# Attention scores as products over 128 rows, with stacked queries and doubled keys

## The chip, the core and the metric

The kernel runs on one core of a Trainium2 chip. Its engines are TensorE (PE in the profile, with its weight loads as PEld), VectorE (DVE), ScalarE (ACT), GpSimd (POOL) and SyncE (SP, which only issues DMAs here). The metric is the device time of one execution in microseconds, the median of some runs.

## What is computed

Two blocks of layers work on 512 positions of width 1024, in float32. The first block has two hybrid layers. Each normalises its input, multiplies it with `w_in`, and runs three kinds of attention over 64-wide heads: differential attention (4 heads with two score maps each), stick-breaking attention (8 heads) and forgetting attention (8 heads). The second block is a float32 mixture: a Hyena layer, an expert layer with 16 experts, a sliding-window attention (SWA) layer with 16 query and 4 key heads, and a second expert layer. Cut to the lines that matter here:

```python
# hybrid layer, query tile i of 128 rows, keys up to its end
s = einsum('bhcqd,bhckd->bhcqk', q[..., q0:q1, :], k[..., :q1, :]) * 64 ** -0.5   # differential
z = einsum('bhqd,bhkd->bhqk', q[:, :, q0:q1], k[:, :, :q1]) * scale               # stick-breaking, forgetting
logits = z + cum_log_f[..., q0:q1, None] - cum_log_f[..., None, :q1]              # forgetting
# SWA, a block of 128 queries: 256 context keys and a band of up to three key blocks
s_ctx = einsum('bqgrd,bkgd->bgrqk', q_b, k_c) * scale
s_loc = einsum('bqgrd,bkgd->bgrqk', q_b, k_b) * scale
```

## The kernel before

**Numbers in two parts.** TensorE multiplies values of a shortened float32 type. Every float32 operand is therefore kept as a high part h and a low part l with h + l = x; `split` (L227 on ACT, L228 on DVE) makes them: ACT copies x into h, DVE subtracts h from x. A product is three matmuls, hh + lh + hl (`mm3`, L93 to L95). The product of the two low parts is left out.

**Scores in the hybrid layers.** A head has 64 features, so a tile of 128 rows holds two heads. `scores` (L584 to L587) takes the 64 rows `rs` of one head and sums four matmuls into one PSUM tile `s`, w = 128, 256, 384 or 512 columns wide for query tile i = 0 to 3; the fourth, over all 128 rows, adds the mask:

```python
nc.tensor.matmul(s[:, :w], q[rs, 0, qs], k[rs, 0, :w], start=True, stop=False)
nc.tensor.matmul(s[:, :w], q[rs, 1, qs], k[rs, 0, :w], start=False, stop=False)
nc.tensor.matmul(s[:, :w], q[rs, 0, qs], k[rs, 1, :w], start=False, stop=False)
nc.tensor.matmul(s[:, i * P:w], self.identr, self.masks[:, mask, :], start=False, stop=True)
```

A layer has 6 units (two of each kind), a unit two pairs of heads, a pair two heads, a head four query tiles: 96 such blocks a layer, 192 in all. The forgetting heads also spread a row of `cum` over 128 rows with a matmul over 40 rows (L690).

**Order of the work in a layer.** `pair(u, j)` projects queries, keys and gates of a pair of heads (24 matmuls of 512 columns each, `proj_f`), splits q and k (L430 and L431, or L227 and L228, after a rotation in `rope_split` for the differential kind) and keeps them in the tiles `q` (3 buffers) and `k` (2). `attend(u, j)` runs scores, softmax and values of that pair. `interleave` weaves the attention of one pair with the projections of the next and the output projection of the unit before (`project_out`). Tile's scheduler then sets each engine's order from these dependencies; every engine works its own list in order.

**Beside it: the adaptive weights.** `between` weaves in `ada_piece`: for the second block's modulation vectors, a 1 MB tile `araw` (one buffer) is loaded on SP's queue, and POOL multiplies its 8 rows with a column and adds them up (L804 once, then L801 and L802 seven times) into `aacc` (4 buffers). There are 24 such sums in layer 0 and 32 in layer 1. `ada_flush` has TensorE turn each `aacc` into a column (`psA`, L821), at a place in TensorE's list that lies up to three sums later. The tile `araw` shares its buffer with the gain rows that a layer's end reads, so the first piece of layer 1 is loaded when layer 0 has ended.

**A layer's end.** `finish` squares, normalises and adds each of the four row tiles (ACT's squares into `xs`, L244, are 128x1024). `xs` lies in the buffers of `q`.

**SWA.** Queries are already stacked there: of a head's 128 rows one half holds the high part, the other the low part, and the keys `kT` stand on both halves. `swa_scores` (L1944, L1945) takes the first product over 128 rows, which gives hh + lh, and the second over the 64 rows of the high part, which gives hl. There are 144 pairs of such matmuls: 96 of 256 columns, 32 of 128, 16 of 512. SWA lies between the two expert layers, whose weights (about 190 MB each) are streamed.

Of the kernel before, what the change touches and what calls it, by code (L numbers as in the profile page):

```python
# [22 lines left out]
P = 128  # L23
D = 1024
S = 512
# [154 lines left out]
class Net:  # L180
# [91 lines left out]
    def first_block(self, before, after, between=lambda n: iter(()), behind=lambda: None):  # L272
# [3 lines left out]
        with ExitStack() as ex:  # L276
            self.pv = self.hx.enter_context(self.pool("pv"))
            self.pA = ex.enter_context(self.pool("pA"))
            pA = self.pA
# [12 lines left out]
            self.sel = pA.tile([40, 8], F32R, name="sel")  # L292
            nc.vector.tensor_tensor(self.sel, self.ident[0:40, 0:8], self.ident[0:40, 32:40], op=ALU.add)
# [32 lines left out]
    def hybrid(self, l, before, after, between):  # L326
# [5 lines left out]
        lv = pA.tile([1, 4, 64], F32, tag="lv", name="lv")  # L332
        nc.sync.dma_start(lv, io["diff_lambda"][l].unsqueeze(0))
        lp = pA.tile([1, 2, 64], F32, tag="lp", name="lp")
# [22 lines left out]
        def forget():  # L357
# [12 lines left out]
            self.cum = pA.tile([40, S], F32R, tag="cum", name="cum")  # L370
# [44 lines left out]
        def pair(u, j):  # L415
# [77 lines left out]
        def finish(tts):  # L493
            for tt in tts:
# [3 lines left out]
                xs = pA.tile([P, D], F32, tag="q", name="xs", bufs=3)  # L498
# [34 lines left out]
    def context_norm(self):  # L533
# [6 lines left out]
        for tt in range(2):  # L540
            x = cx[:, tt, :]
            scr = self.pA.tile([P, D], F32, tag="q", name="cs", bufs=3)
# [22 lines left out]
    def rope_split(self, dst, a):  # L565
# [10 lines left out]
        self.split(dst[:, 0, :], dst[:, 1, :], t1)  # L576

    def scores(self, q, k, r0, i, mask):
# [3 lines left out]
        rs = slice(r0, r0 + 64)  # L582
# [40 lines left out]
    def diff_head(self, q, k, vt, j, gt, sub, nlam, y):  # L623
# [4 lines left out]
        def exps(i):  # L628
            w = (i + 1) * P
            e, zs = [], []  # L630
            for c in range(2):
                s = self.scores(q, k, 64 * c, i, 0)
# [44 lines left out]
    def pair64(self, kind, q, k, vt, j, gt, y, head0, groups):  # L677
# [6 lines left out]
        def exps(hh, g, i):  # L684
            w = (i + 1) * P
            if kind == "f" and i == groups[0][0]:
                n = cols.stop
                cb = self.ps.tile([P, S], F32, tag="s", name="cb", bufs=3)
                sel = self.sel[:, head0 + hh:head0 + hh + 1].to_broadcast([40, P])
# [1458 lines left out]
```

## Time and profile before

| | |
|---|---|
| median of 3 runs | 3364.06 us (3361.09 to 3375.61) |
| the profiled execution | 3359.41 us |
| its span, first to last instruction | 3357.5 us |
| hybrid layer 0, layer 1 | about 150 to 680, 680 to 1250 us |
| SWA attention | about 2540 to 2800 us |
| busy: PE, DVE, ACT, POOL | 2995.8, 2215.3, 1504.6, 1103.9 us |

The durations below belong to the profiled execution. Busy times of PE overcount, because the end of a matmul is modelled and successive ones overlap: the distance from start to start is what a matmul costs the engine. Waits are named by what came last. TensorE's clock is 2.4 GHz at a granted share of 1.00 and 1.2 GHz at 0.50.

### The profile page before, as it was taken

The page shows a single profiled execution, that of the slowest core. Times are in us where ns is not written, and L with a number is a line of the kernel's source. Part 1 is how long each engine was busy: PE and PEld are TensorE (multiplying, and loading weights), DVE is VectorE, ACT ScalarE, POOL GpSimd, SP SyncE. Part 2 cuts the span into 40 slices and gives each one's busy share as a digit, 9 for nine tenths or more (in the row PEclk, how much of TensorE's full clock was granted, in tenths as well). Part 3 has the DMA queues.
Part 4 walks back from the last instruction along what each step waited for, and adds up shares of the span by engine and source line. Part 5 has one row for each costly group of instructions (what it writes and reads, how often), then busy time and mean ns, then how long its engine had stood idle before and what let it go on. Part 6 is the DMA issues. An engine that isn't in the chain of part 4 may idle for free. (4 is left out here: it accounts for less than half of the span.)

```text
span 3357.5 us, 42248 instructions
## 1 busy us (share of the span) xinstructions
PE 2995.8 (89%) x15148; PEld 2169.4 (65%) x15148; DVE 2215.3 (66%) x4023; ACT 1504.6 (45%) x2649; POOL 1103.9 (33%) x1310
## 2 busy tenths in 40 slices
PE   7999999899999988998886999999798995976776
PEld 4777778687777768888775677766576773322222
DVE  8676776776677588878867899998776665100002
ACT  5345664544465353332322788877654652000001
POOL 4374665167766622113332012120203231000000
PEclk9999999999899989999997999999997987998988
DMA  5432222323233334553466999999431016999996
GB/s 175 150 112 89 79 91 82 120 95 107 88 126 114 126 114 135 163 163 115 154 221 259 335 387 382 390 373 366 148 107 58 13 51 255 403 403 404 404 398 267
DMA packets 289513, 673.23 MB, mean 201 GB/s; under 512 B 16352, under 2 KB 151759, under 8 KB 289304
## 3 DMA queue, kind: packets, MB, share of 16 engines
q1 hardware_dynamic: 267592, 604.50, 49.1%
q0 software_dynamic: 18256, 58.70, 5.9%
q10 hardware_dynamic: 3456, 7.34, 0.6%
q8 instruction: 120, 1.97, 0.2%
q14 instruction: 89, 0.73, 0.1%
HBM read 618.49 MB, written 51.99 MB: 200 GB/s over the span
## 5 line engine op out<-in xcount | busy, mean ns | idle before, releaser
L228 DVE TENSOR_TENSOR mwl<-raww,mwh 128x1024 fp32r<-128x1024 f32 x384 | 461.3, 1226 | 56.9 <-ACT mwh L227 53.9
L227 ACT ACTIVATE mwh<-raww 128x1024 fp32r<-128x1024 f32 x384 | 405.2, 1060 | 147.1 <-PE psg L94 61.9
L802 POOL TENSOR_TENSOR aacc<-aacc,aprod 128x256 f32<-128x256 f32 x392 | 328.7, 839 | 31.7
L1503 PE MATMUL psg<-raww,xt 128*64 128x512 f32 x1024 | 259.4, 649 | 88.5 <-DMA raww<-in_moe_w_gate_dram 48.5
L801 POOL TENSOR_SCALAR aprod<-araw,cvec 128x256 f32<-128x256 f32 x392 | 259.0, 661 | 64.5 <-DMA araw<-in_ada_w_dram 29.8
L1528 DVE TENSOR_TENSOR a<-psg,a 128x512 f32<-128x512 f32 x16 | 11.1, 692 | 362.8 <-ACT a L1527 362.8
L1503 PEld LDWEIGHTS psg<-raww,xt 128*64 128x64 f32 x1024 | 73.6, 147 | 261.1 <-issue 136.9
L93 PE MATMUL acc<-hTh,wh 128*128 128x512 f32 x576 | 231.8, 402 | 0.0
L94 PE MATMUL acc<-hTh,wl 128*128 128x512 f32 x576 | 227.7, 395 | 1.5 <-DVE wl L228 1.5
L95 PE MATMUL acc<-hTl,wh 128*128 128x512 f32 x576 | 227.8, 396 | 0.0
L1527 ACT ACTIVATE a<-psg 128x512 f32<-128x512 f32 x16 | 9.6, 597 | 364.7 <-PE psg L1503 364.7
L228 DVE TENSOR_TENSOR wl<-raw,wh 128x1024 fp32r<-128x1024 f32 x106 | 140.4, 1325 | 42.3 <-ACT wh L227 42.3
L1440 POOL DMA_INDIRECT xe<-hrows,idx x16 | 21.5, 1345 | 390.8 <-PE psC L1432 366.6
L1518 POOL DMA_INDIRECT xe<-hrows,idx x16 | 15.7, 983 | 355.8 <-PE psC L1510 319.9
L1503 PE MATMUL psd<-raww,at 128*64 128x512 f32 x512 | 118.1, 609 | 13.5 <-DVE ye L1540 8.2
L227 ACT ACTIVATE wh<-raw 128x1024 fp32r<-128x1024 f32 x106 | 111.6, 1053 | 30.9 <-PE accv L94 19.7
L94 PEld LDWEIGHTS acc<-hTh,wl 128*128 128x128 f32 x576 | 109.0, 189 | 21.5 <-DVE wl L228 2.1
L95 PEld LDWEIGHTS acc<-hTl,wh 128*128 128x128 f32 x576 | 108.7, 189 | 21.8
L93 PEld LDWEIGHTS acc<-hTh,wh 128*128 128x128 f32 x576 | 109.0, 189 | 19.9 <-issue 0.4
L93 PE MATMUL accv<-wvh,hTh 128*128 128x256 f32 x384 | 111.7, 291 | 0.0
L94 PE MATMUL accv<-wvh,hTl 128*128 128x256 f32 x384 | 110.9, 289 | 0.7 <-DVE hTl L228 0.7
L95 PE MATMUL accv<-wvl,hTh 128*128 128x256 f32 x384 | 109.8, 288 | 0.3 <-DVE wvl L228 0.3
(631 smaller groups left out, 8995.0 us busy)
## 6 DMA issues: line engine op xcount, KB each, us to landing
raww<-in_moe_w_gate_dram SPq DMA_DIRECT2D x128, 1024.0 KB, 9.9
raww<-in_moe_w_up_dram SPq DMA_DIRECT2D x127, 1024.0 KB, 10.8
raww<-in_moe_w_down_dram SPq DMA_DIRECT2D x125, 1024.0 KB, 18.5
raw<-in_w_in_dram SPq DMA_DIRECT2D x48, 1024.0 KB, 5.5
araw<-in_ada_w_dram SPq DMA_DIRECT2D x36, 1024.0 KB, 5.0
spec<-sp SPq DMA_DIRECT2D x24, 512.0 KB, 3.1
rawo<-in_w_out_dram SPq DMA_DIRECT2D x12, 1024.0 KB, 7.2
raw<-in_hy_w_in_dram SPq DMA_DIRECT2D x12, 1024.0 KB, 5.3
```

What stands on the lines that cost most here:

```text
L93: nc.tensor.matmul(out, ah, bh, start=start, stop=False)
L94: nc.tensor.matmul(out, al, bh, start=False, stop=False)
L95: nc.tensor.matmul(out, ah, bl, start=False, stop=stop)
L227: self.split_act = self.nc.scalar.activation(h, src, AF.Copy).ins
L228: (eng or self.nc.vector).tensor_tensor(l, src, h.bitcast(F32), op=ALU.subtract)
L801: nc.gpsimd.tensor_scalar(prod, raw[:, c, :], col, 0.0, op0=ALU.mult, op1=ALU.add)
L802: nc.gpsimd.tensor_tensor(acc, acc, prod, op=ALU.add)
L1440: m.gather = nc.gpsimd.indirect_dma_start(out=xe, out_offset=None, in_=m.hrows[:, :], in_offset=bass.IndirectOffsetOnAxis(ap=idx[:, e:e + ...
L1503: nc.tensor.matmul(out[64 * hf:64 * hf + 64], lhs[:, c % 4, 64 * (c // 4):64 * (c // 4) + 64], raw[:, cc, hf * 512:hf * 512 + 512], start= ...
L1518: m.gather = nc.gpsimd.indirect_dma_start(out=xe, out_offset=None, in_=halves(m.hrows), in_offset=bass.IndirectOffsetOnAxis(ap=idx[:, e:e ...
L1527: self.last_other = nc.scalar.activation(a, gu[:, 0, :], AF.Silu).ins
L1528: nc.vector.tensor_tensor(a, gu[:, 1, :], a, op=ALU.mult)
```

## The change

- In the hybrid layers `stack` writes the queries of each head over all 128 rows, the high part on the head's own 64 rows and the low part on the other 64, and `twice` writes each head's keys on both halves, high and low. `scores` then takes two matmuls over 128 rows and the mask: (h; l) against kh, and (h; l) against kl, which also adds the product of the low parts.
- `q` has 2 buffers in place of 3; `k` has twice the size. `cum` and `sel` have 128 rows.
- In SWA the second product is taken over 128 rows, too.
- To make room, `lo` goes: the scratch half is kept in `yv`. `lv`, `lp` and `hrow` move into the buffers of `x`; `xs` (a layer's end) and `pp` (Hyena) move from the buffers of `q` to those of `y`, the attention outputs that the last output projection reads.

```diff
-            self.cum = pA.tile([40, S], F32R, tag="cum", name="cum")
+            self.cum = pA.tile([P, S], F32R, tag="cum", name="cum")
...
-            q = pA.tile([P, 2, S], F32R, tag="q", name="q", bufs=3)
-            k = pA.tile([P, 2, S], F32R, tag="k", name="k", bufs=2)
+            q = pA.tile([P, 2, S], F32R, tag="q", name="q", bufs=2)
+            k = pA.tile([P, 2, 2, S], F32R, tag="k", name="k", bufs=2)
...
                 if kind == "a":
-                    self.rope_split(dst, a)
-                elif n == 0:
-                    nc.scalar.activation(dst[:, 0, :], a, AF.Copy, scale=0.125)
-                    nc.vector.scalar_tensor_tensor(dst[:, 1, :], a, 0.125, dst[:, 0, :].bitcast(F32),
-                                                   op0=ALU.mult, op1=ALU.subtract)
+                    a = self.roped(dst if n == 0 else dst[:, 0], a)
+                if n == 0:
+                    self.stack(dst, a, None if kind == "a" else 0.125)
                 else:
-                    self.split(dst[:, 0, :], dst[:, 1, :], a)
+                    self.twice(dst, a)
...
-                xs = pA.tile([P, D], F32, tag="q", name="xs", bufs=3)
+                xs = pA.tile([P, D], F32, tag="y", name="xs", bufs=3)
...
+    def stack(self, q, a, scale=None):
+        for i in range(2):
+            h, l = slice(64 * i, 64 * i + 64), slice(64 - 64 * i, 128 - 64 * i)
+            nc.scalar.activation(q[h, i, :], a[h], AF.Copy, scale=1.0 if scale is None else scale)
+            if scale is None:
+                nc.vector.tensor_tensor(q[l, i, :], a[h], q[h, i, :].bitcast(F32), op=ALU.subtract)
+            else:
+                nc.vector.scalar_tensor_tensor(q[l, i, :], a[h], scale, q[h, i, :].bitcast(F32),
+                                               op0=ALU.mult, op1=ALU.subtract)
+    def twice(self, k, a):
+        for i in range(2):
+            h, o = slice(64 * i, 64 * i + 64), slice(64 - 64 * i, 128 - 64 * i)
+            self.split(k[h, i, 0, :], k[h, i, 1, :], a[h])
+            if i == 0:
+                nc.scalar.activation(k[o, i], k[h, i].bitcast(F32), AF.Copy)
+            else:
+                nc.vector.tensor_copy(k[o, i], k[h, i].bitcast(F32))
...
-        nc.tensor.matmul(s[:, :w], q[rs, 0, qs], k[rs, 0, :w], start=True, stop=False)
-        nc.tensor.matmul(s[:, :w], q[rs, 1, qs], k[rs, 0, :w], start=False, stop=False)
-        nc.tensor.matmul(s[:, :w], q[rs, 0, qs], k[rs, 1, :w], start=False, stop=False)
+        for x in range(2):
+            nc.tensor.matmul(s[:, :w], q[:, hh, qs], k[:, hh, x, :w], start=x == 0, stop=False)
...
-            lo = pA.tile([P, S], F32, tag="lo", name="lo", bufs=1)
-            nc.scalar.activation(lo[0:64, cols], o[64:128, cols], AF.Copy)
-            nc.vector.tensor_tensor(yv[rows, cols], o[0:64, cols], lo[0:64, cols], op=ALU.add)
+            nc.scalar.activation(yv[64:128, cols], o[64:128, cols], AF.Copy)
+            nc.vector.tensor_tensor(yv[rows, cols], o[0:64, cols], yv[64:128, cols], op=ALU.add)
...
-            nc.tensor.matmul(o, q[rq, r, qs], kT[rq, g, 1, ks], start=False, stop=n + k == len(order) or n + k == 4)
+            nc.tensor.matmul(o, q[:, r, qs], kT[:, g, 1, ks], start=False, stop=n + k == len(order) or n + k == 4)
```

Since a scheduler sets the order, the built programs were compared, too. Three places matter. TensorE's list, layer 0, unit 0, second pair, last query tile (`s` is a score block, `acc` a projection, `psP` a transpose, `psA` one of the adaptive columns); before:

```order
L95 MATMUL acc<-hTl,wh 128x512
L584 MATMUL s<-k,q 128x512
L585 MATMUL s<-k,q 128x512
L586 MATMUL s<-k,q 128x512
L587 MATMUL s<-masks,identr 128x128
L93 MATMUL acc<-hTh,wh 128x512
```

After:

```order
L93 MATMUL acc<-hTh,wh 128x512
L606 MATMUL s<-k,q 128x512 x2
L607 MATMUL s<-masks,identr 128x128
L606 MATMUL s<-k,q 128x512 x2
L607 MATMUL s<-masks,identr 128x128
L640 MATMUL psP<-ident,e 128x128 x2
```

A block is three matmuls where it was four; the two heads' blocks now follow each other here. Of the 56 adaptive columns of the two layers, each stands behind the same share of the score blocks as before, to about 1 in 100.

ACT's list, layer 0, unit 3, keys of the first pair (`k<-acc` is the high part, `wh` a weight split, `e` softmax, `pt` a transposed weight tile, `sg` the gate); before:

```order
L701 ACTIVATE e<-e,one 128x512
L227 ACTIVATE k<-acc 128x512
L227 ACTIVATE wh<-raw 128x1024
L742 ACTIVATE lo<-o 64x512
L227 ACTIVATE pt<-psP 128x2x128
```

After:

```order
L721 ACTIVATE e<-e,one 128x512
L227 ACTIVATE k<-acc 64x512
L227 ACTIVATE wh<-raw 128x1024
L761 ACTIVATE yv<-o 64x512
L583 ACTIVATE k<-k 64x1024
L227 ACTIVATE k<-acc 64x512
L227 ACTIVATE pt<-psP 128x2x128
L736 ACTIVATE e<-e 128x512
L557 ACTIVATE sg<-acc 128x512
```

One operation has become three, and the copy of the first head's keys (L583) needs DVE's subtraction first. On DVE one subtraction has become two and a copy (CAST `k<-k 64x1024`). On TensorE, in all 24 pairs, at least 28 matmuls (the 24 of the gate's projection among them) stand between the end of the keys' projection and the first score that reads them.

ACT's list at the end of layer 0 (`xs,ss` is a square, `y` the last attention output, `yv` or `lo` its halves, `wvh` a weight split for layer 1); before:

```order
L244 ACTIVATE xs,ss<-yacc 128x1024
L227 ACTIVATE y<-yv 128x128
L233 ACTIVATE rs<-ss,eps 128x1
L235 ACTIVATE rs<-rs 128x1
L244 ACTIVATE xs,ss<-yacc 128x1024
L742 ACTIVATE lo<-o 64x128
```

After:

```order
L244 ACTIVATE xs,ss<-yacc 128x1024
L227 ACTIVATE y<-yv 128x128
L233 ACTIVATE rs<-ss,eps 128x1
L235 ACTIVATE rs<-rs 128x1
L761 ACTIVATE yv<-o 64x128 x2
L227 ACTIVATE y<-yv 128x128
L227 ACTIVATE wvh<-raw 128x1024
L244 ACTIVATE xs,ss<-yacc 128x1024 x2
```

The squares of the second and third row tile have moved behind the last attention output and a weight split. SP's and POOL's lists of loads and sums keep their order but for single rows; POOL's 448 multiplications and additions of layer 1 are the same.

## Rows read from the trace of the kernel before

**Rows 1.** By stretch: us, busy (count) of PE, PEld, DVE, ACT, POOL; PEclk, DMA share, GB/s.

```profile
150.00:600.00 450.00, 444.73 (x2369) 354.78 (x2368) 320.59 (x666) 240.95 (x498) 270.10 (x366) 1.00 0.30 94
690.00:1180.00 490.00, 468.17 (x2403) 371.46 (x2403) 323.55 (x658) 242.23 (x498) 351.20 (x480) 0.96 0.34 111
2580.00:2700.00 120.00, 115.10 (x595) 84.83 (x594) 83.49 (x266) 78.03 (x198) 40.60 (x41) 0.99 0.05 19
```

**Rows 2.** Timeline of PE, blocks of 512 columns: start, duration in us, line, operands.

```profile
803.21 0.50 PE L584 MATMUL s<-k,q 64*128 64x512 f32 x1
803.56 0.39 PE L585 MATMUL s<-k,q 64*128 64x512 f32 x1
803.79 0.39 PE L586 MATMUL s<-k,q 64*128 64x512 f32 x1
804.11 0.33 PE L587 MATMUL s<-masks,identr 128*128 128x128 f32 x1
804.37 0.49 PE L584 MATMUL s<-k,q 64*128 64x512 f32 x1
```

**Rows 3.** Timeline of PE, score blocks of 128 columns.

```profile
785.60 0.32 PE L584 MATMUL s<-k,q 64*128 64x128 f32 x1
785.76 0.27 PE L585 MATMUL s<-k,q 64*128 64x128 f32 x1
785.88 0.27 PE L586 MATMUL s<-k,q 64*128 64x128 f32 x1
...
786.34 0.33 PE L584 MATMUL s<-k,q 64*128 64x128 f32 x1
```

**Rows 4.** Timeline of PE, SWA: score products, then products with the values.

```profile
2600.18 0.38 PE L1945 MATMUL sc<-kT,qw 64*128 64x256 f32 x1
2600.49 0.39 PE L1944 MATMUL sc<-kT,qw 128*128 128x256 f32 x1
2600.81 0.38 PE L1945 MATMUL sc<-kT,qw 64*128 64x256 f32 x1
...
2602.09 0.28 PE L1845 MATMUL ow<-ptl,vt 128*128 128x256 f32 x1
2602.21 0.28 PE L1845 MATMUL ow<-pth,vt 128*128 128x256 f32 x1
```

**Rows 5.** Groups on DVE, 60 to 1250 us: form, count, busy us, mean ns, idle before.

```profile
L228 DVE TENSOR_TENSOR wl<-raw,wh 128x1024 fp32r<-128x1024 f32 x73 | 98.0, 1343 | 40.2 <-ACT wh L227 40.2
...
L228 DVE TENSOR_TENSOR k<-acc,k 128x512 fp32r<-128x512 f32 x24 | 16.4, 685 | 25.6 <-ACT k L227 25.6
```

**Rows 6.** The same on ACT.

```profile
L227 ACT ACTIVATE k<-acc 128x512 fp32r<-128x512 f32 x24 | 14.3, 597 | 37.5 <-PE acc L95 37.4
...
L244 ACT ACTIVATE xs<-yacc 128x1024 f32<-128x1024 f32 x11 | 11.6, 1053 | 5.6 <-DVE yacc L503 4.3 <-DVE yacc L475 1.0 <-PE psT L251 0.3
```

**Rows 7.** Groups on POOL, 690 to 1180 us.

```profile
L802 POOL TENSOR_TENSOR aacc<-aacc,aprod 128x256 f32<-128x256 f32 x223 | 184.7, 828 | 18.1
L801 POOL TENSOR_SCALAR aprod<-araw,cvec 128x256 f32<-128x256 f32 x222 | 149.1, 672 | 23.8 <-DMA araw<-in_ada_w_dram 4.3
L804 POOL TENSOR_SCALAR aacc<-araw,cvec 128x256 f32<-128x256 f32 x30 | 16.2, 541 | 93.4 <-DMA araw<-in_ada_w_dram 80.5 <-PE s L587 4.3 <-PE o L734 4.3
```

**Rows 8.** Waits of POOL, 150 to 640 us: total us, times, longest.

```profile
POOL aacc L804 <- PE psA L821: 69.4, 8, 21.3
```

**Rows 9.** Waits of PE, 690 to 1240 us.

```profile
PE psA L821 <- POOL aacc L802: 15.6, 4, 6.6
```

**Rows 10.** Timeline of POOL, layer 1.

```profile
700.97 1.85 POOL L801 TENSOR_SCALAR aprod<-araw,cvec 128x256 f32<-128x256 f32 x1
```

**Rows 11.** Timeline of DVE at that time.

```profile
701.34 1.21 DVE L228 TENSOR_TENSOR wl<-raw,wh 128x1024 fp32r<-128x1024 f32 x1
```

**Rows 12.** By stretch, around a wait of PE for POOL in layer 1.

```profile
819.00:825.00 6.00, 0.80 (x5) 0.58 (x4) 1.38 (x3) 2.28 (x3) 5.37 (x8) 0.94 0.00 0
825.00:834.00 9.00, 8.89 (x31) 7.03 (x32) 4.53 (x14) 2.67 (x7) 4.34 (x8) 0.50 0.75 235
```

More of the change, by code (lines that the diff above doesn't have):

```diff
@@ L290, in first_block @@
             nc.sync.dma_start(self.rope, io["k_rope"].rearrange("m p f -> p m f"))
-            self.sel = pA.tile([40, 8], F32R, name="sel")
-            nc.vector.tensor_tensor(self.sel, self.ident[0:40, 0:8], self.ident[0:40, 32:40], op=ALU.add)
+            self.sel = pA.tile([P, 8], F32R, name="sel")
+            nc.vector.tensor_tensor(self.sel, self.ident[:, 0:8], self.ident[:, 32:40], op=ALU.add)
             self.meanw = pA.tile([P, P], F32, name="meanw")
@@ L329, in hybrid @@
         lam_init = 0.8 - 0.6 * math.exp(-0.3 * l)
-        lv = pA.tile([1, 4, 64], F32, tag="lv", name="lv")
+        lv = pA.tile([1, 4, 64], F32, tag="x", name="lv", bufs=3)
         nc.sync.dma_start(lv, io["diff_lambda"][l].unsqueeze(0))
-        lp = pA.tile([1, 2, 64], F32, tag="lp", name="lp")
+        lp = pA.tile([1, 2, 64], F32, tag="x", name="lp", bufs=3)
         lm = pA.tile([1, 4], F32, tag="lm", name="lm")
@@ L541, in context_norm @@
             x = cx[:, tt, :]
-            scr = self.pA.tile([P, D], F32, tag="q", name="cs", bufs=3)
+            scr = self.pA.tile([P, D], F32, tag="q", name="cs", bufs=2)
             r = self.rownorm(self.pA, x, scr)
@@ L563, in silu, with roped @@
         nc.vector.tensor_tensor(out, g, t, op=ALU.mult)
-    def rope_split(self, dst, a):
+    def stack(self, q, a, scale=None):
+        nc = self.nc
+        for i in range(2):
[7 more added lines that the diff above has]
+    def twice(self, k, a):
+        nc = self.nc
+        for i in range(2):
[5 more added lines that the diff above has]
+                nc.vector.tensor_copy(k[o, i], k[h, i].bitcast(F32))
+    def roped(self, dst, a):
         nc, pA = self.nc, self.pA
@@ L575, in rope_split, with scores @@
         nc.vector.tensor_tensor(t1, t1, t2, op=ALU.add)
-        self.split(dst[:, 0, :], dst[:, 1, :], t1)
-    def scores(self, q, k, r0, i, mask):
+        return t1
+    def scores(self, q, k, hh, i, mask):
         nc = self.nc
@@ L631, in exps @@
             for c in range(2):
-                s = self.scores(q, k, 64 * c, i, 0)
+                s = self.scores(q, k, c, i, 0)
                 e.append(pA.tile([P, S], F32, tag="e", name="e", bufs=4))
@@ L688, in exps @@
                 cb = self.ps.tile([P, S], F32, tag="s", name="cb", bufs=3)
-                sel = self.sel[:, head0 + hh:head0 + hh + 1].to_broadcast([40, P])
+                sel = self.sel[:, head0 + hh:head0 + hh + 1].to_broadcast([P, P])
                 nc.tensor.matmul(cb[:, :n], sel, self.cum[:, :n], start=True, stop=True)
@@ L692, in exps @@
                 nc.scalar.activation(st["cum"][:, :n], cb[:, :n], AF.Copy)
-            s = self.scores(q, k, 64 * hh, i, 1 if kind == "s" else 2)
+            s = self.scores(q, k, hh, i, 1 if kind == "s" else 2)
             e = pA.tile([P, S], F32, tag="e", name="e", bufs=4)
@@ L1041, in hyena_cols @@
         nc, io = self.nc, self.io
-        rows = p.tile([P, S], F32, tag="lo", name="hrow", bufs=1)[:120, :P]
+        rows = p.tile([P, S], F32, tag="x", name="hrow", bufs=3)[:120, :P]
         srcs = [io["hy_b_in_2"]] + [io["hy_short_w_2"][i] for i in range(3)] + [io["hy_short_b_2"]]
@@ L1072, in shorts @@
             ch = h2 // P
-            pp = p.tile([P, D], F32, tag="q", name="pp", bufs=3)
+            pp = p.tile([P, D], F32, tag="y", name="pp", bufs=3)
             nc.gpsimd.memset(pp[:, 0:1], 0.0)
@@ L1933, in swa_scores @@
         qs = slice(i * P, i * P + P)
-        rq = slice(64 * r, 64 * r + 64)
         pieces = []
```

1 line of the change is left out of this document (removed).

## Prediction, made before the changed kernel ran

> **What bounds the kernel now.** I read three things in this order: the busy times by stretch, then the timeline of TensorE for what a score block really costs, then POOL's groups and waits, because POOL's sums feed TensorE. In layer 0 of the hybrid part TensorE is busy 444.7 of 450 us, DVE 320.6 and ACT 241.0 [rows 1]. PE's share is overcounted, since matmuls overlap, but it waits for little there: POOL waited 69.4 us for TensorE to free a sum's buffer [rows 8], so POOL runs ahead. Layer 0 is bound by TensorE. Layer 1 looks alike by stretch (468.2 of 490 us [rows 1]), but its POOL is in another state. Its three groups are busy 184.7 + 149.1 + 16.2 = 350.0 us and idle 18.1 + 23.8 + 93.4 = 135.3 us before them [rows 7], together 485 of 490 us. The idle time is the loads of `araw` (80.5 + 4.3 us named so) and small steps between operations; none of it is named as a wait for a column. At 8.6 us of it a PE line is named, in stretches of 4.3 us, as long as a load. TensorE, on the other hand, waited 15.6 us for POOL's sums [rows 9]. So in layer 1 a chain of loads and sums on POOL is already as long as TensorE's list, and TensorE touches it. In SWA TensorE is the fullest engine (115.1 of 120 us, overcounted), with DVE at 83.5 and ACT at 78.0 [rows 1]. The expert layers and Hyena are not touched; they start when what stands ahead of them ends, so I let a gain ahead of them pass through whole.
>
> **What a score block costs.** From start to start, a block of 512 columns takes 804.37 - 803.21 = 1.16 us [rows 2]. Its second 64-row product takes 0.23 us, but the first 0.35 and the third 0.32, and the mask 0.26. The extra time stands where TensorE passes from 64 to 128 rows or back, or changes the rows. A block of 128 columns takes 0.74 us, of which the second product is 0.12 [rows 3]. Products over 128 rows that follow each other show no such extra: 256 columns take 0.12 us [rows 4], half of the 0.23 for 512.
>
> **The new block.** It is two products and a mask, all over 128 rows. For 512 columns I take 0.23 + 0.23 + 0.12 = 0.58 us, a saving of 0.58; for 128 columns 3 x 0.12 = 0.36, a saving of 0.38. The two middle widths are put on the line between, 0.45 and 0.51. The mean is 0.48 us, times 192 blocks 92 us, 46 a layer. If the extra time did not depend on the rows at all, only one product a block would go: (0.12 + 0.12 + 0.18 + 0.23) / 4 = 0.16 us, 31 us in both layers. These are the two ends; I take the upper, because the second product in each block shows the bare pace.
>
> **What is added.** In each of the 12 pairs of a layer q and k each get a second split. On DVE that is 2 x 0.685 us, since half the rows at the same 512 columns is taken to last as long as the whole [rows 5]; on ACT 2 x 0.597 [rows 6]. Each gets a copy of 64x1024 besides: on DVE between 0.69 (a pass over 512) and 1.34 (over 1024) [rows 5], I take 1.0; on ACT up to 1.2. That is 12 x 2.4 = 28 us on either engine in a layer. In the stretch of 450 us, DVE goes from 71% to about (320.6 + 26) / (450 - 42) = 85%, ACT to about 65%. It lies beside TensorE's work: behind the keys' projection at least 28 matmuls stand ahead of the first score that reads those keys, 24 of them of 512 columns, 24 x 0.23 = 5.5 us. The keys' chain, two splits and a copy in a row, is 2 x (0.60 + 0.69) + 1.2 = 3.8 us, and up to 5.1 with the copy on DVE behind it, where it was 1.3. The cover holds by little, and what is queued ahead on DVE comes on top. The change adds a wait, too: ACT's copy of the first keys waits for DVE's subtraction, and behind it on ACT stand the second head's keys, a transposed tile `pt` and the gate; TensorE waits for `pt`. So I let TensorE realise three quarters in layer 0: 46 x 0.75 = 34 us. The ends are all 46 (every wait hidden) and 16 (about a third, DVE setting the pace).
>
> **The ends of the layers.** The squares of the second and third tile now wait until the last output projection has read its `y`: two passes of about 1.05 us [rows 6] that ran ahead before. I take 2 us a layer, between 0 and 4. Smaller edits (`yv` as scratch, two buffers of `q`, where `k` had two before, `lv` and `hrow` in other buffers, 128 rows for `cum`) I cost at nothing: buffers of `x` and `q` are free by then, as the work that reads them stands ahead; without that cover each would be one pass of 0.7 us.
>
> **Layer 1.** TensorE saves the same 46 us but cannot use it. The sums keep their places among its matmuls, and POOL's chain of 485 us starts when layer 0 has ended. At most 490 - 485 = 5 us are to be had up to the last sum. Behind it stands a twentieth of the layer's score blocks, 2 us, which the layer's end takes back. So 5 us. The ends are 34 (POOL is no bound) and -16 (POOL slowed, below).
>
> **SWA.** A pair of products of 256 columns takes 2600.81 - 2600.18 = 0.63 us and would take 0.24 [rows 4]: 0.39 us saved, for 144 pairs 56 us, taking the other widths alike. In the stretch of 120 us some 75 pairs lie, 29 us. With those gone TensorE needs 91 at most, and DVE's 83.5 us come next, so the whole is out of reach: I take two thirds, 37 us, between 14 (a quarter) and 56.
>
> **Sum.** Layer 0 34 - 2 = 32, layer 1 5, SWA 37: 74 us. The profiled execution took 3359.4 us and would take 3285; the median of the runs lies 4.7 us above it, so 3364.1 - 74 = 3290 us.
>
> **Rivals.**
>
> *POOL is no bound in layer 1* (its loads come earlier, or the sums are wanted later). Then layer 1 gains as layer 0, 32 for 5: 101 us, 3263. For it: TensorE waited only 15.6 us so far. Against: 485 of 490 us, and a list of sums that keeps its order. 0.15.
>
> *DVE takes over.* It goes to 85% in layer 0 and above 90% in SWA, in order, with chains both ways. Layer 0 gives 16 - 2, layer 1 3, SWA 14: 31 us, 3333. For it are the added 28 us a layer; against, that today's DVE at 71% makes TensorE wait for little. 0.17.
>
> *POOL is slowed by DVE.* A sum's multiplication takes 0.67 us on average, but 1.85 us [rows 10] while DVE subtracts two tiles from the buffer memory [rows 11]. The 12 new copies a layer on DVE read and write that memory; if each holds POOL up for 1.34 us, its chain in layer 1 grows by 16 us, which TensorE can't hide: 58 us gained, 3306. 0.10. The Trainium skill, "SBUF — State Buffer", section "SBUF: two separate sides", says that VectorE and GpSimd share a pair of ports that one holds alone for a whole instruction, and counts a float32 copy within SBUF among the instructions that take it. By that rule this rival would be the forecast; the row agrees with the rule for a subtraction, and no row shows a copy.
>
> *The change doesn't do what it says*: the extra time stays and only the third product goes. Then layer 0 gives 15.5 x 0.75 - 2 = 10, layer 1 3, SWA nothing: 13 us, 3351. Against it are the bare 0.23 and 0.12 us. 0.04.
>
> *Slower: the clock falls where TensorE waits for POOL.* After a wait of some 5.6 us the granted clock was 0.50, 1.2 GHz, for about 9 us [rows 12], which costs 4.5 us of work. TensorE's list in layer 1 is 490 - 15.6 - 46 = 428 us. Were there such a drop at each of the 32 sums, it would be 428 + 32 x 4.5 = 572, 82 us longer than now, and against the 69 us won elsewhere the kernel would take 3377. It turns slower than before from (490 + 69 - 428) / 4.5 = 29 drops on. Against it: a slow TensorE falls behind POOL and has nothing to wait for, so the drops limit themselves. 0.03.
>
> **How the numbers follow.** The forecast, layer 1 held by POOL and the rest won in part, has 0.51. A measurement of this kernel tells about 0.5% (17 us) from no change, so faster means below 3347. The forecast, the first and third rival and nearly all of the second lie there: 0.90. Within 0.5% are the fourth and a rest of the second: 0.07. Slower is the last: 0.03. The range leaves out the last two, and the tails of the first two: 3250 to 3335.
>
> **What would show it.** In the profile after: score blocks of 512 columns some 0.58 us apart, and SWA pairs some 0.24. Layer 0 shorter by 25 to 40 us. Layer 1, from its first sum on POOL to its last, as long as now, with TensorE's wait for POOL up from 15.6 to about 50 us; this is the step that I would look at first, for if it is wrong, layer 1 is shorter by 30. New rows on DVE and ACT of 64 rows with 0.6 to 0.7 us, and copies of 1.0 to 1.3. SWA shorter by 25 to 50, with DVE ahead of TensorE in more waits. The prediction is wrong as a whole if the products over 128 rows show gaps of 0.3 us too, or if waits for DVE grow by tens of us in layer 0.

## The result, and the profile of the changed kernel

The changed kernel takes 3312.45 us (median of 4 runs, 3310.67 to 3314.22), the kernel before 3364.94: 52.5 us less, a ratio of 0.9839 with an interval of 0.9816 to 0.9862. The forecast was 3290 with a range of 3250 to 3335. The direction and the range held; of the 74 us that were forecast, 52 came. The profiled execution has a span of 3312.0 us, 45.5 less than the one before, and the sums below are made in these 45.5.

**Where they lie.** Four marks divide the program: POOL's first sum of layer 1, the end of its last one, and the starts of the first and last product of SWA.

| stretch | before | after | won | forecast |
|---|---|---|---|---|
| up to layer 1's first sum | 684.9 | 669.5 | 15.4 | 32 |
| layer 1, first sum to last | 490.5 | 500.3 | -9.8 | 5 |
| from there to SWA's first score product | 1364.5 | 1365.8 | -1.4 | 0 |
| SWA, first score product to last product with the values | 248.8 | 206.5 | 42.3 | 37 |
| the rest | 568.8 | 569.9 | -1.1 | 0 |

The stretches of the kernel after, columns as in [rows 1]: the differential heads of layer 0, the rest of layer 0 up to its last sum, layer 1, and a part of SWA. They answer to [rows 1].

```profile
160.00:332.00 172.00, 161.62 (x859) 137.03 (x857) 129.18 (x268) 95.19 (x183) 106.60 (x136) 0.96 0.29 94
332.00:574.00 242.00, 234.82 (x1369) 199.87 (x1368) 202.11 (x405) 164.99 (x340) 177.75 (x226) 1.00 0.30 96
669.00:1170.00 501.00, 439.99 (x2357) 375.34 (x2356) 351.72 (x691) 268.69 (x532) 365.35 (x484) 0.93 0.32 107
2580.00:2690.00 110.00, 97.12 (x625) 81.65 (x624) 92.04 (x278) 81.27 (x211) 43.05 (x42) 0.98 0.08 30
```

The first two stretches in the kernel before, for comparison:

```profile
160.00:332.00 172.00, 170.46 (x890) 136.51 (x888) 119.51 (x257) 83.29 (x168) 103.39 (x137) 1.00 0.30 94
332.00:600.00 268.00, 264.89 (x1441) 210.69 (x1441) 195.51 (x393) 154.28 (x325) 165.77 (x226) 1.00 0.28 91
```

Read them with the ends of the stretches in mind. In the differential heads TensorE was busy for all but 1.5 of 172 us before; after, it has 10 us of holes in the same 172, while DVE went from 119.5 to 129.2 us. The rest of the layer, up to the last sum, takes 242 us instead of 268. The granted clock of the differential heads went from 1.00 to 0.96. In layer 1 TensorE is busy 440 of 501 us, at a granted clock of 0.93.

**The score blocks** did what was forecast. The timeline of PE, a pair of hybrid blocks of 512 columns (two products printed as one line), and SWA's pairs of 256 columns:

```profile
787.33 0.62 PE L606 MATMUL s<-k,q 128*128 128x512 f32 x2
787.79 0.22 PE L607 MATMUL s<-masks,identr 128*128 128x128 f32 x1
787.95 0.73 PE L606 MATMUL s<-k,q 128*128 128x512 f32 x2
...
2569.08 0.28 PE L1962 MATMUL sc<-kT,qw 128*128 128x256 f32 x1
2569.20 0.28 PE L1963 MATMUL sc<-kT,qw 128*128 128x256 f32 x1
2569.32 0.28 PE L1962 MATMUL sc<-kT,qw 128*128 128x256 f32 x1
```

The two blocks shown start 787.95 - 787.33 = 0.62 us apart; the median of the 45 blocks of 512 that the trace holds whole is 0.57, against 0.58 in the prediction, and a SWA pair takes 2569.32 - 2569.08 = 0.24 us, as forecast.

**Layer 1's chain on POOL**, first sum to last; the columns are those of [rows 7]. First before (the same groups as [rows 7], over the whole chain), then after. The idle time of the last line holds one wait ahead of the first sum, 25.0 us before and 19.4 after, which is not part of the chain.

```profile
L802 POOL TENSOR_TENSOR aacc<-aacc,aprod 128x256 f32<-128x256 f32 x224 | 186.4, 832 | 18.1
L801 POOL TENSOR_SCALAR aprod<-araw,cvec 128x256 f32<-128x256 f32 x224 | 150.9, 674 | 23.9 <-DMA araw<-in_ada_w_dram 4.3
L804 POOL TENSOR_SCALAR aacc<-araw,cvec 128x256 f32<-128x256 f32 x32 | 17.2, 537 | 118.4 <-DMA araw<-in_ada_w_dram 105.5 <-PE s L587 4.3 <-PE o L734 4.3
```

```profile
L821 POOL TENSOR_TENSOR aacc<-aacc,aprod 128x256 f32<-128x256 f32 x224 | 185.4, 828 | 18.1
L820 POOL TENSOR_SCALAR aprod<-araw,cvec 128x256 f32<-128x256 f32 x224 | 156.3, 698 | 23.9 <-DMA araw<-in_ada_w_dram 4.3
L823 POOL TENSOR_SCALAR aacc<-araw,cvec 128x256 f32<-128x256 f32 x32 | 22.6, 708 | 112.6 <-DMA araw<-in_ada_w_dram 103.6 <-PE o L754 4.9 <-PE acco L95 4.1
```

The idle time within the chain is 135 us in both. The busy time grew from 354.5 to 364.3 us: that is the whole of the 9.8 us by which layer 1 got longer. Not all of it need be the change: in swa_only (experiment 4), whose hybrid layers are written as before, the chain took 495.1 us with 359.0 us busy. None of the chain's idle time is named as a wait for TensorE to free a sum. And the wait of PE for these sums, against 15.6 us in 4 waits in [rows 9] (here total, times, longest):

```profile
PE psA L840 <- POOL aacc L821: 44.1, 13, 9.1
```

**The end of layer 0.** At the layer's last sum the changed kernel is 26.9 us ahead (TensorE takes it at 572.5 instead of 599.4 us), at the first sum of layer 1 only 15.4. Between them lies this, in the timeline of POOL and then of PE:

```profile
594.42 0.28 POOL L343 PARTITION_BROADCAST nlam<-lm  x1 [15.13 <-DVE lm L341]
608.64 0.53 POOL L371 MEMSET cum<- 128x512 f32 x1 [13.94 <-PE cb L710]
616.80 4.65 POOL L228 TENSOR_TENSOR wol<-rawo,woh 128x1024 fp32r<-128x1024 f32 x2 [7.63 <-issue]
```

```profile
610.90 0.73 PE L94 MATMUL acco<-woh,y 128*128 128x512 f32 x2
619.18 1.22 PE L95 MATMUL acco<-wol,y 128*128 128x512 f32 x2 [7.55 <-POOL wol L228]
```

`nlam` is the lambda of the *second* layer. Its row `lv` sits in a buffer of tag `x` now and is loaded only when one comes free, so its broadcast has slid from 305 us to 594, to a place right ahead of the last split of the output weights, which POOL does. Behind the broadcast POOL's next TENSOR instruction starts 7.6 us late with nothing recorded in between; TensorE waits 7.55 us for the split. The clock fell with that wait, as the stretches show (columns as above; the seventh number is PEclk):

```profile
594.00:611.00 17.00, 16.96 (x98) 14.33 (x96) 15.16 (x52) 11.05 (x27) 0.81 (x2) 1.00 0.09 27
611.00:620.00 9.00, 1.45 (x4) 0.91 (x5) 3.04 (x10) 2.15 (x6) 3.20 (x2) 0.62 0.10 41
620.00:634.00 14.00, 13.08 (x56) 11.47 (x56) 7.47 (x19) 4.91 (x13) 1.46 (x1) 0.63 0.25 76
```

### The profile page after: what moved, and what is told of

It is laid out like the page before. It is cut to its first block, busy times and chain, and to the rows that moved or that the text cites. A ratio compares the mean times of both kernels' runs of the same rounds, so it can differ in the third digit from the quotient of the medians.

```text
span 3312.0 us, 41976 instructions
## 1 busy us (share of the span) xinstructions
PE 2865.1 (87%) x14956; PEld 2148.0 (65%) x14956; DVE 2274.0 (69%) x4095; ACT 1551.9 (47%) x2721; POOL 1126.8 (34%) x1310
## 5 line engine op out<-in xcount | busy, mean ns | idle before, releaser
L820 POOL TENSOR_SCALAR aprod<-araw,cvec 128x256 f32<-128x256 f32 x392 | 279.9, 714 | 63.8 <-DMA araw<-in_ada_w_dram 29.0
L94 PE MATMUL acc<-hTh,wl 128*128 128x512 f32 x576 | 229.1, 398 | 1.8 <-DVE wl L228 1.8
L95 PE MATMUL acc<-hTl,wh 128*128 128x512 f32 x576 | 229.3, 398 | 0.0
L95 PEld LDWEIGHTS acc<-hTl,wh 128*128 128x128 f32 x576 | 109.9, 191 | 22.8
L94 PEld LDWEIGHTS acc<-hTh,wl 128*128 128x128 f32 x576 | 110.0, 191 | 22.3 <-DVE wl L228 2.4
L94 PE MATMUL accv<-wvh,hTl 128*128 128x256 f32 x384 | 113.9, 297 | 2.8 <-DVE rs L234 2.8
L95 PE MATMUL accv<-wvl,hTh 128*128 128x256 f32 x384 | 113.3, 297 | 2.1 <-DVE wvl L228 2.1
```

Source lines behind the costliest of these rows:

```text
L94: nc.tensor.matmul(out, al, bh, start=False, stop=False)
L95: nc.tensor.matmul(out, ah, bl, start=False, stop=stop)
L820: nc.gpsimd.tensor_scalar(prod, raw[:, c, :], col, 0.0, op0=ALU.mult, op1=ALU.add)
```

## The experiments

**1. Is it the lambda's buffer?** The changed kernel with a buffer of its own for `lv` (the products of its rows are written into it, too):

```
-        lv = pA.tile([1, 4, 64], F32, tag="x", name="lv", bufs=3)
+        lv = pA.tile([1, 4, 64], F32, tag="lv", name="lv")
-        lp = pA.tile([1, 2, 64], F32, tag="x", name="lp", bufs=3)
```

> The changed kernel, but the row for the lambda of the second layer (lv) has its own buffer again, and its products are written into it, instead of waiting for a buffer of tag x. Theory: the wait of TensorE for the low half of the last output weights in layer 0 (7.6 us, behind a 7.6 us step of POOL that follows the lambda's broadcast) and the low clock after it go, and with them 8 to 13 us: 3300 to 3305. Rival (the 11 us that layer 0 loses at its end come from the later squares or from DVE): within 3 us of the changed kernel, 3310 to 3315.

Measured: 3305.7 us, ratio 0.9813 (0.9784 to 0.9842), 6.8 us below the changed kernel and 1 us short of what was expected. The intervals of the two ratios overlap; the single runs (3304.5 to 3308.6 and 3310.7 to 3314.2) do not. The broadcast is back at 306 us, and the split follows the memset at once:

```profile
306.65 0.79 POOL L342 PARTITION_BROADCAST nlam<-lm  x1 [6.88 <-DVE r L661]
314.47 0.47 POOL L822 TENSOR_SCALAR aacc<-araw,cvec 128x256 f32<-128x256 f32 x1 [7.02 <-issue]
...
609.09 0.53 POOL L370 MEMSET cum<- 128x512 f32 x1 [29.13 <-PE cb L709]
609.58 4.78 POOL L228 TENSOR_TENSOR wol<-rawo,woh 128x1024 fp32r<-128x1024 f32 x2
```

The 7 us behind the broadcast are paid at 306 us too, where POOL has time to spare. Layer 1's first sum comes 4.8 us earlier (664.7). The rival, that the whole loss is DVE's or the squares', falls; but less than half of the 11.5 us that the layer's end lost comes back there. Of the rest 3.5 us are the squares (below). For the other 3 us no run has a single cause, but right behind the split the trace has something that was not there before (a row of DVE, one of PE, and a stretch):

```profile
612.08 2.82 DVE L228 TENSOR_TENSOR y<-yv,y 128x512 fp32r<-128x512 f32 x1
```

```profile
614.96 1.22 PE L94 MATMUL acco<-woh,y 128*128 128x512 f32 x2 [3.61 <-DVE y L228]
```

```profile
614.00:624.00 10.00, 8.12 (x29) 7.11 (x30) 6.71 (x17) 3.35 (x8) 0.36 (x1) 0.50 0.36 107
```

DVE's subtraction of `y` starts while POOL's split runs and takes 2.82 us, where it took 0.68 before. TensorE waits 3.6 us for it, and the granted clock behind that is 0.50 for 10 us; before, TensorE had no such wait here, and the clock stayed at 1.00. So a wait and a low clock remain at this place without the broadcast, and only a part of the drop shown above is the broadcast's.

**2. Does POOL's chain set layer 1?** Two of layer 1's 24 pieces of ada columns are moved to layer 0, in the changed kernel and in the kernel before:

```
-  6 * x // 5 if x < 10 else 12 + 12 * (x - 10) // 5
+  7 * x // 5 if x < 10 else 14 + 11 * (x - 10) // 5
```

> The changed kernel with two of the 24 pieces of ada columns moved from layer 1 to layer 0 (14 and 22, so 28 sums in each layer instead of 24 and 32). Theory (POOL's chain sets layer 1): a sum costs POOL some 12.7 us and a piece's load 3.9, so the chain of layer 1 goes from 500 to some 441 us and TensorE's wait for sums from 44 to under 10; layer 0's chain of some 410 us still fits its 423. The kernel gains 30 to 45 us: 3268 to 3283. Rival (layer 1 is held by DVE or by waits between the engines, and POOL only follows): under 10 us, 3303 to 3315.

> The kernel before with the same two pieces moved. Theory: POOL only touched TensorE there (15.6 us of waits), so it gains 5 to 20 us: 3345 to 3360, and the change, measured between the two balanced kernels, is worth 70 to 90 us instead of 52. Rival (POOL's chain doesn't decide in either kernel): both balanced kernels move alike, and the change is still worth 45 to 58 us.

Measured: balance 3280.6 us, ratio 0.9739 (0.9710 to 0.9768); balance_before 3351.8, ratio 0.9949 (0.9930 to 0.9967). Layer 1's chain is 442.2 us (441 were expected), and the 44 us of TensorE's waits for POOL's sums have gone down to 3.0. One wait of 15.9 us at a column is put down to DVE, but DVE and ACT stand idle there as well, until a tile of output weights lands; SP, which issues in order, has three loads of `araw` ahead of it, each of which needs the one buffer that POOL reads (rows of SP, then of ACT):

```profile
1029.20 30.70 SPq L810 DMA_DIRECT2D araw<-in_ada_w_dram  x3
1059.98 0.53 SPq L457 DMA_DIRECT2D rawo<-in_w_out_dram  x1
```

```profile
1067.49 1.06 ACT L227 ACTIVATE woh<-rawo 128x1024 fp32r<-128x1024 f32 x1 [18.93 <-DMA rawo<-in_w_out_dram]
```

So the single buffer of `araw` can hold up the other loads, too. Layer 0 pays for the move: its last sum comes at 595.4 instead of 572.5. The numbers of POOL's theory are the ones that came: 32 us for the changed kernel, 13 to 17 for the one before, and the change between the two balanced kernels is worth 71 us.

**3. Is it POOL's waiting or its work?** A piece is loaded into two buffers of half the size, so that a half is loaded while POOL works on the other; every sum is made as before and where it was. The two gain rows of a layer's end, which share these buffers, become two tiles for it.

```
-  raw = pool.tile([P, NC, 256], F32, tag="araw", name="araw", bufs=1)
-  nc.sync.dma_start(raw, ...)
+  raws = [pool.tile([P, 4, 256], F32, tag="araw", name="araw", bufs=2) for _ in range(2)]
+  for h in range(2):
+      nc.sync.dma_start(raws[h], src[:, 4 * h:4 * h + 4, :])
```

> The changed kernel, with each piece of ada weights loaded into two buffers of half the size instead of one, so that a half can be loaded again while POOL works on the other. No sum is moved and no work is left out. Theory (POOL's chain of loads and sums sets layer 1): of its 500 us some 84 are waits for loads, which go, and TensorE's wait for sums (44 us) goes with them; what is left is TensorE's own list of some 455 us. 30 to 45 us less than the changed kernel: 3268 to 3283. Rival (in the balanced kernel it was the work, 46 us less of it in layer 1, that gave DVE and the memory port room): under 15 us, since POOL's work stays.

> The same with the lambda's own buffer as well. If the two are independent the gains add: 7 us less than with the halved loads alone, 3260 to 3276. If layer 1 hides what layer 0 wins, the time is that of the halved loads alone within 3 us.

> The kernel before with the halved loads of the ada weights, nothing else. Theory (the lock of layer 1 by POOL is what kept the change from showing): before, TensorE waited only 15.6 us for sums, and the clock fell after some of the waits, so 15 to 25 us are to be had: 3340 to 3350. Against the changed kernel with halved loads and its own lambda buffer (3246.7) the change is then worth 92 to 103 us, near to the 101 us that the prediction gave for a layer 1 without the lock. Rival (the halved loads help both kernels alike): 3300 to 3312, the change worth 55 to 65.

Measured: halved_loads 3254.2 us, ratio 0.9667 (0.9647 to 0.9686), 58 us below the changed kernel, more than the 30 to 45 expected; with the lambda's buffer 3246.7, ratio 0.9639 (0.9622 to 0.9655), so 7.4 us more, and the two gains add. The kernel before with halved loads: 3332.8, ratio 0.9916 (0.9899 to 0.9932), some 28 to 31 us less, and not 15 to 25. POOL's groups and waits in halved_loads, layer 1 (12.5 us of the waits for loads include 11.4 ahead of the first sum):

```profile
L824 POOL TENSOR_TENSOR aacc<-aacc,aprod 128x256 f32<-128x256 f32 x224 | 196.7, 878 | 17.5
L823 POOL TENSOR_SCALAR aprod<-araw,cvec 128x256 f32<-128x256 f32 x224 | 158.3, 707 | 22.6 <-DMA araw<-in_ada_w_dram 1.1
L826 POOL TENSOR_SCALAR aacc<-araw,cvec 128x256 f32<-128x256 f32 x32 | 19.5, 611 | 29.3 <-PE psA L843 15.5 <-DMA araw<-in_ada_w_dram 12.5 <-PE accv L95 0.9
```

POOL's work did not shrink (374.5 us busy instead of 364.3); its chain did, to 432.8 us, and now it is POOL that waits for TensorE to take a sum (15.5 us). The rival, that less work on POOL was what helped, is out. What was worth more than expected is the clock. With halved loads the granted clock of layer 1 in the changed kernel is 0.97 (660 to 1105 us) instead of 0.93. In the kernel before, layer 1's granted clock was 0.96 ([rows 1]); in halved_before it is 0.99:

```profile
681.00:1141.00 460.00, 451.50 (x2420) 362.70 (x2418) 324.19 (x649) 239.93 (x490) 359.61 (x484) 0.99 0.36 115
```

A mean of 0.96 over 490 us means 8% of the time, 39 us, at 0.50, and so some 20 us of work lost; 0.99 over 460 us loses 5. The 15 us between them and the 15.6 us of waits make the 30. The expectation had counted the waits and only a little of the clock.

Between halved_before and halved_loads_lambda, two kernels in which POOL's chain no longer holds layer 1, the change is worth 86 us by the medians and 93 by the ratios. The expectation said 92 to 103, and the rival 55 to 65; the rival is out, and the expectation was a little high.

**4. SWA alone.** The kernel before with one line changed:

```
-  nc.tensor.matmul(o, q[rq, r, qs], kT[rq, g, 1, ks], ...)
+  nc.tensor.matmul(o, q[:, r, qs], kT[:, g, 1, ks], ...)
```

> The kernel before with only the second score product of SWA over 128 rows. Theory: 38 to 45 us less than before, 3320 to 3327, the whole of the 42 us by which SWA is shorter in the changed kernel. Rival (part of that comes from the hybrid layers' new buffers or from DVE's order): 20 to 35 us.

Measured: 3322.3 us, ratio 0.9860 (0.9830 to 0.9890), 43 us less than the median of the kernel before given above and 47 by the ratio. SWA, from its first score product to its last product with the values, takes 209.0 us, 39.8 less than before (in the changed kernel 206.5). The timeline of PE:

```profile
2542.74 0.58 PE L1943 MATMUL sc<-kT,qw 128*128 128x256 f32 x1 [1.43 <-DVE t L1698]
...
2751.71 0.27 PE L1847 MATMUL ow<-ident,rec 128*128 128x128 f32 x1
```

So this line brought 39.8 of the 42.3 us that SWA won, and most of what the whole change won; the new layout of the hybrid layers, with all its splits and copies, brought the other 7 to 10 us.

**5. Rows or number of products?** A third product over 128 rows in every score block of the hybrid layers:

```
-  for x in range(2):
+  for x in (0, 1, 1):
```

> The changed kernel with three products over 128 rows in a score block of the hybrid layers instead of two (the second is made twice, so the scores' small terms count double). Theory (a product over 128 rows among others costs its bare pace, 0.12 to 0.23 us, and the saving is the missing product and the extra time at the changes of rows, both): a block of 512 columns takes 0.80 us instead of 0.57, layer 0 gets some 12 to 16 us longer, and layer 1 hides it behind POOL: 3322 to 3332. Rival (the number of products decides, and the rows cost nothing): 0.57 + 0.58 = 1.15 us a block as before, layer 0 loses the whole 26 us that it had won: 3335 to 3345.

> The changed kernel with the third product over 128 rows once more, for its profile; its time was 3315.5, 3 us above the changed kernel and below the 12 to 16 that were expected. Theory now: a block of 512 columns takes 0.80 us as expected, but in the differential heads of layer 0 (the first 180 us of it), where TensorE in the changed kernel waits 23 us in small steps for the softmax on DVE and ACT, it only fills those waits; so layer 0's last sum comes 3 to 8 us later there and layer 1 takes it back. Rival: the third product costs less than its pace (under 0.1 us), so the blocks are as long as with two.

Measured: 3315.5 us, ratio 0.9856 (0.9839 to 0.9872), and in the second run 3311.1, ratio 0.9845 (0.9825 to 0.9865): the third product costs nothing that can be measured, where the first expectation said 10 to 20 us. The profile of the second run shows that it does take its time (timeline of PE, three products printed as one line, and the layer's last sum):

```profile
797.36 0.95 PE L606 MATMUL s<-k,q 128*128 128x512 f32 x3
798.14 0.22 PE L607 MATMUL s<-masks,identr 128*128 128x128 f32 x1
798.20 0.91 PE L606 MATMUL s<-k,q 128*128 128x512 f32 x3
...
580.93 0.50 PE L840 MATMUL psA<-one,aacc 128*128 128x1 f32 x4
```

The median of 40 blocks of 512 columns is 0.80 us, as expected, and each product keeps its 0.23. An old block, with its 64-row products, has a median of 1.056 us (the one in [rows 2] took 1.16), a new one 0.573, and one with three products 0.800. So of the 0.48 us that such a block won, the missing product made 0.23, and the changes between 64 and 128 rows 0.26. A new block also keeps one and the same query operand for all its products, where the old one changed it; that is not what the 0.26 us are, for products over 128 rows that change one operand or both follow each other at the bare pace ([rows 4]: 0.12 us for 256 columns with `ptl` and `pth`; the projections: a median of 0.227 us for 512 from L94 to L95). Layer 0's last sum comes 8.4 us later (580.9 for 572.5), just above the 3 to 8 that were expected the second time. The differential heads swallow their share (they end at 331.5 us for 330.9); and in layer 1 TensorE's wait for POOL falls from 44 to 27 us and gives the rest back. That is POOL's hold on layer 1 seen from its other side: more work for TensorE costs nothing there either. Part of it is luck of the order too: here the lambda's broadcast does not delay the output weights.

**6. The doubled keys' copies.** On ACT alone (in the changed kernel, and in the one with halved loads and lambda's buffer), and on DVE alone (in the latter):

```
-  if i == 0:
-      nc.scalar.activation(k[o, i], k[h, i].bitcast(F32), AF.Copy)
-  else:
-      nc.vector.tensor_copy(k[o, i], k[h, i].bitcast(F32))
+  nc.scalar.activation(k[o, i], k[h, i].bitcast(F32), AF.Copy)    (or nc.vector.tensor_copy)
```

> The changed kernel with both copies of the doubled keys on ACT instead of one on ACT and one on DVE. Theory (from the trace: 9 of POOL's operations in layer 1 met such a copy and took 0.3 us longer each): POOL's chain in layer 1 gets 2 to 4 us shorter than 500, the kernel moves by under 5 us: 3308 to 3316. Rival (a copy of DVE holds POOL for its whole length, 12 of 0.8 us, so it explains the 10 us by which the chain is longer than before): the chain falls to some 490 us, and the kernel to 3300 to 3305.

> The kernel with halved loads and the lambda's buffer (3246.7), with both copies of the doubled keys on DVE instead of one on ACT. Both copies on ACT had made layer 0 some 5 us longer. Theory (the differential heads wait for the shorter of the hand-overs, and ACT's copy of 1.06 us stands in ACT's list ahead of the softmax): 5 to 12 us less, 3235 to 3242. Rival (DVE, with more work than ACT in every stretch, is what the heads wait for): 3250 to 3262.

> The kernel with halved loads and the lambda's buffer (3246.7), with both copies of the doubled keys on ACT. Both on DVE had cost 19 us. Theory (DVE is what the heads wait for, and ACT has room): the 12 copies of 0.8 us a layer leave DVE, and 3 to 12 us are won, 3235 to 3244. Rival (the two copies run side by side when they are shared, and one engine alone makes the keys' chain longer, whichever it is): 3249 to 3262.

Measured: copies_on_act 3312.0 us, ratio 0.9836 (0.9819 to 0.9852), no difference; copies_on_dve 3265.8, ratio 0.9712 (0.9696 to 0.9728), 19 us more than 3246.7; halved_copies_act 3248.9, ratio 0.9671 (0.9642 to 0.9700), no difference. Adding work to DVE costs, adding it to ACT does not: the theory of copies_on_dve, that ACT was the engine that is waited for, fell. Its rival (DVE is what the heads wait for) had the direction, but 3265.8 is above its 3250 to 3262, and the differential heads end where they did (331.6 us for 331.5). The rest of layer 0 pays, its last sum at 584.9 instead of 572.9, and some 7 us are lost behind layer 1's last sum. But taking the copies off DVE brings nothing either (the 3 to 12 us expected of halved_copies_act did not come). That the split between the two is already as good as ACT alone is what was measured; why is open.

For POOL, copies_on_act says this: its busy time in layer 1's chain goes back to 355.9 us (354.5 before, 364.3 after), the chain only to 496.4. That is the 2 to 4 us of its theory; the rival (490, and 3300 to 3305 for the kernel) is out. How a copy meets POOL shows in the timeline of the changed kernel:

```profile
723.97 0.73 POOL L821 TENSOR_TENSOR aacc<-aacc,aprod 128x256 f32<-128x256 f32 x1
724.35 0.90 DVE L585 CAST k<-k 64x1024 fp32r<-64x1024 f32 x1
724.80 0.80 POOL L820 TENSOR_SCALAR aprod<-araw,cvec 128x256 f32<-128x256 f32 x1
725.68 0.74 POOL L821 TENSOR_TENSOR aacc<-aacc,aprod 128x256 f32<-128x256 f32 x1
```

The copy takes 0.90 us where it takes 0.69 alone: it starts under a running sum, and the product behind takes 0.80 instead of 0.48. Of the 12 copies in layer 1, 9 met POOL so, and by the trace cost it 0.32 us each, 2.9 us in all. The other 7 of the 10 us are POOL operations that met DVE's older instructions more often (the splits of the output weights 3.3 us more, the scans 2.4 more); that these meetings went away with the copies as well is a matter of how the lists came to lie, which no run here tells further; and 4.5 us of busy time more than before stood in swa_only, too, which has no such copies.

## Why the prediction was right, and where it was not

**The score block: right.** 0.57 and 0.24 us for 0.58 and 0.24. The saving was put a little high, since the old blocks were read off single rows: over the 167 old and 183 new blocks that the traces hold whole the old medians are 0.64, 0.71, 0.89 and 1.06 us and the new ones 0.33, 0.30, 0.41 and 0.57, a mean saving of 0.42, which is 40 us a layer, not 46.

**Layer 0, 34 us: the term was too large.** Up to the last sum 26.9 us came. None of them came in the differential heads: the last of their squares' products stands at 330.7 us before and at 330.9 after. Measured from start to start of the matmuls against the median of their kind, TensorE's bare work there went from 163 to 146 us, and its pauses from 7 to 23. Some 10 us of them are waits, small and with many names (the largest, `psP` for DVE's `e`, 3.4 us in 3 waits), so no single wait took the saving's place. Some 7 us are the clock, which the prediction had no term for here: a mean of 0.96 over 172 us, reckoned as in experiment 3, is 14 us at 0.50. What holds this stretch is open: that product stands at 330 to 333 us in every trace here, with a third product in each block and with both copies on DVE as well. The rest of the layer won 27.1 us, all that its 64 blocks gave (64 x 0.42 = 27). "Three quarters" was thus a mean over a part that gives nothing and a part that gives everything. The second rival, DVE taking over, is borne out only in small: TensorE's waits put down to DVE in layer 0 grew from 3.6 to 12.9 us, and not by the tens that were to show it. DVE is at 75% in those heads, and more work for it (experiment 6) lengthens the rest of the layer, where the whole saving came, and not them.

**The smaller edits, costed at nothing: wrong.** The sentence said that buffers of `x` are free by then. `lv` does get one, but late, and the price was not a pass of 0.7 us: it was the place to which the broadcast moved, with 7.6 us of TensorE behind it and 14 us at a clock of 0.63 (a part of which stays without it, experiment 1). The order of the changed program has the broadcast there, and the prediction did not look for it. The price, by the two kernels with a buffer of its own, is 6.8 to 7.4 us.

**The squares, 2 us: right in kind.** The first turn of the next layer's input now waits 7.30 us for them, 3.83 before, so 3.5 us, inside the 0 to 4. At the end of layer 1 the same kind of turn waits 14.0 us for POOL's `xs`, 7.0 before; that is more than the 4, and what of it is the squares no run tells. The rows are of PE, layer 0, before and after:

```profile
665.78 1.97 PE L251 MATMUL psT<-ident,xs 128*128 128x128 f32 x8 [3.83 <-DVE xs L305]
```

```profile
647.94 1.97 PE L251 MATMUL psT<-ident,xs 128*128 128x128 f32 x8 [7.30 <-DVE xs L305]
```

**Layer 1: the mechanism was right, and it is what the runs bear out best.** POOL's chain of loads and sums held the layer; TensorE's wait rose to 44 us (50 were forecast) and the layer won nothing. The term was off by 15 us: +5 was forecast and -9.8 came. The 9.8 us are POOL's longer busy time. The third rival (DVE's copies slow POOL by 16 us in this layer) is true in kind, beside the forecast and not instead of it: the copies' meetings are 2.9 us, and 4.5 us lie within what two chains without copies differ by (before and swa_only). The Trainium skill, "SBUF — State Buffer", section "SBUF: two separate sides", says that DVE or GpSimd holds the shared ports for a whole instruction and the other blocks. The timeline above agrees, in both directions; but a meeting cost POOL 0.32 us, not the copy's 0.7 to 0.9, since in that timeline each of the two waits at most for what is left of the other's instruction.

**SWA, 37 us: a little low.** 42 of the 56 us came, three quarters instead of two thirds. (The narrow and the wide pairs save less than 0.39 us each; by the medians of each width the 56 are 53.) DVE did become the fuller neighbour (92 of 110 us), and TensorE's two longest kinds of wait for it rose from 10.3 to 18.9 us.

**The rival with the clock** was right in its mechanism (13 waits instead of 4, and 0.93 for 0.96) and, as its argument against it said, the drops limited themselves: layer 1 grew by 9.8 us and not by 82, and no wait of POOL's chain is for a sum that TensorE still had to take. Where POOL does not hold the layer, the clock is half of the price: in halved_before it doubled what the waits were worth.

**What the whole is worth.** 45.5 us of span as it was made, 83 between the spans of the two kernels with halved loads (3330.2 and 3247.3, the second with lambda's buffer). That is the first rival's case, which said 101 us: 24 us came up to layer 1's first sum (32 were said), 17 from there to SWA (32) and 43 in SWA (37); behind it 2 were lost. So even without POOL's hold layer 1 gave only half of what was said. The best kernel run here is halved_loads_lambda, 3246.7 us, 66 below the changed one; it does all the work, and the step that brought most of it is one that a look at POOL's 85 us of waits for its own loads offers, before the change as after.

## What to carry to other kernels

Before shortening an engine's list, lay the chain that feeds it beside it, idle time included: where the two are equally long, the gain needs both, and a buffer cut in two can be all that the feeder needs. An edit that gives a small tile a shared buffer moves that tile's whole chain to where the buffer comes free; look in the order for what lands behind it, above all behind an instruction that leaves its engine a delay, as the broadcast does here. A wait of TensorE costs more than its own length: here, where POOL did not hold the layer, the work lost at the lower clock behind the waits was about as much again.

## What the runs showed of the hardware that was not expected

After a PARTITION_BROADCAST, POOL's next TENSOR instruction started 6.7 to 8.2 us late in every trace (but where it waited longer for something else), with no instruction recorded in the time; a MEMSET in between was not delayed (608.64 us above), the TENSOR_TENSOR behind it was. The Trainium skill, "GPSIMD Engine Reference", section "2.1 Instruction dispatch", says that the first call of a freshly loaded kernel pays some 6 us, and that no instruction shows it. The rows agree with the second half, and give 7 to 8 us here; that the delay is such a first call, no run shows.

A product over 128 rows between others of its kind costs 0.23 us for 512 columns whether it is the second or the third of a block; a block with three products over 64 rows takes 0.26 us more than one with three over 128 (1.056 and 0.800, medians), which is what the changes between 64 and 128 rows cost.
